# A mixer's products with ones and zeros, split into two float32r parts, and a looser order of weight splits

## The chip, the cores and the metric

The kernel runs on one core of a Trainium2 chip. The metric is the device time of one launch in microseconds; lower is better. TensorE multiplies, VectorE and ScalarE do elementwise work and read the products out of PSUM, SyncE issues nearly all loads from device memory.

## The reference

One transformer block on 256 tokens of width 2048, in float32, batch 1. A conditioning vector gives nine modulation vectors (`w_ada`). Three sublayers follow, each with a norm before and after and a residual: a gated feed-forward net (width 5632), a hybrid mixer, and a second feed-forward net. The mixer is

```python
p = h @ w_in
y_pool = multiscale_pool(p[..., :POOL_WIDTH], pool_w, pool_scale)
y_rwkv = rwkv7_time_mix(p[..., POOL_WIDTH:], mu_shift, w0, w2, a0, a2, g2, k_k, k_a, r_k, lnx_w, lnx_b)
return jnp.concatenate([y_pool, y_rwkv], axis=-1) @ w_out
```

`rwkv7_time_mix` has 24 heads of 64 channels. Sums over the 64 channels of a head occur three times: in the norm of `kk`, in the bonus (the sum of `r * k * r_k`, times `v`), and in the mean and variance of each head's output. Between them a recurrence runs over the tokens, with a state of 64x64 per head.

## The kernel before, in words

Tokens lie along the free dimension, channels on the 128 partitions; one 128-row tile holds two heads. Large products are made with weights in two float32r parts: `split` (L181) lets ScalarE copy a raw weight tile to `hi` (L187) and VectorE compute `lo = raw - hi` (L188); three matmuls, `hi` by the activation's high part, `hi` by its low part and `lo` by its high part, stand for one product (`mm3` L207, `rows_mm`). There are four `hi` and `lo` buffers in the mixer and four raw ones; a raw buffer is free for its next load when `lo` is made.

Other products of the mixer are plain float32. Four of them for each group multiply data of 128x512 by a constant of ones and zeros, so as to sum over the channels of a head (`blocks`) or over blocks of 8 (`same`): the norm (`ns`, from `sq`), the bonus (from `rk`), the diagonal of small triangular blocks (`same`, from `dg`), and the variance (in `rwkv_b`, from another `sq`). In the trace the first two write the bank `ga` from tiles named `y` and `t`, the third writes `sa` from `pm`, the fourth `sb` from `t`; all four read `consts`.

The recurrence is done in chunks of 64 tokens, for six groups of four heads. `rwkv_a` (L1117) prepares a group, `rwkv_b` (L1260) solves it; both are generators that yield at fixed places. `stage` (L931) runs 12 slots for each group: in each slot first two pieces of weight work (`pieces`: the projection of the next group, a piece being one split and its matmuls), then the end of the group before last (`b_old`), then a segment of `rwkv_b` for the previous group, a segment of `rwkv_a` for this group (slots 0, 2, 4, 5, 6, 7, 9), other tasks, and a part of the conditioning sums (`ada`). In `rwkv_a`, `sq` and `rk` are made in slot 0, the norm's product stands in slot 2, the bonus in slot 4, `dg` is made in slot 7 and multiplied in slot 9. TensorE's instructions are bound to exactly this order (`ordered`, `pe` L197); those of the other engines are ordered by a scheduler by priority and its own estimates, then each engine runs its list in order. `mark` names an operation that later `ada` sums have to follow.

After group 5 a last stage runs with `rwkv_b` alone, at 1.5 pieces a slot; these are pieces of `w_out` (six matmuls of 512 columns each). Only there `act_linked` is set: several copies of `rwkv_b` out of PSUM go through `link` (L385), and every later weight split's cast must follow the last of them:

```python
def link(self, op):
    if self.act_linked:
        self.act_link = op
    return op
...
    if self.act_link is not None:            # in split
        self.after(a, self.act_link, "order")
```

The linked copies are `Z0` (twice), `pm`, `X`, `Q` and the square before the variance, in slots 1, 3, 4, 5, 6 and 10. The bonus's result is read by `bv` (L1192), which frees bank `ga` for the matmuls `ga<-ar,bk` of the next slot; these need `ar` (L1181 and L1182).

Of the kernel before, what the change touches and what calls it, by code (L numbers as in the profile page):

```python
# [11 lines left out]
F32 = mybir.dt.float32  # L12
F32R = mybir.dt.float32r
AF = mybir.ActivationFunctionType
ALU = mybir.AluOpType
PSUM = bass.MemoryType.PSUM

P = 128
T = 256
# [23 lines left out]
C = 64  # L43
H = C // 2
NC = T // C
U = 2 * NC
B = 8
LOG_DECAY = -float(np.exp(-0.5))

CONST_LAYOUT = (("ident", P), ("quads", 32), ("blocks", P), ("center", C), ("tri", P), ("gmask", P),  # L50
                ("lmask", 2 * H), ("hmask", 2), ("eye", C), ("recip", 4 * 16),
                ("same", P), ("bmask", C // B), ("b32mask", H // B), ("imask", B))


def constant_pack():
    p, f = np.arange(P)[:, None], np.arange(P)[None, :]
    q, j = p % C, np.arange(C)[None, :]
    same = (p // C == f // C).astype(np.float32)
    levels = []
    o, i = p % H, np.arange(H)[None, :]  # L60
    for s in (8, 16):
        levels.append((o == i) | ((o // (2 * s) == i // (2 * s)) & (o % (2 * s) >= s) & (i % (2 * s) < s)))
    recip = np.concatenate([1.0 / np.minimum(np.arange(1, 17), w) for w in POOL_WINDOWS])
    parts = {
        "ident": p == f,
        "quads": p % 32 == np.arange(32)[None, :],
        "blocks": same,
        "center": (q == j) - 1.0 / C,
        "tri": same * (p <= f) * LOG_DECAY,
        "gmask": np.concatenate([q < j, q <= j], 1),  # L70
        "lmask": np.concatenate(levels, 1),
        "hmask": q // H == np.arange(2)[None, :],
        "eye": q == j,
        "recip": np.broadcast_to(recip, (P, 64)),
        "same": p // B == f // B,
        "bmask": q // B == np.arange(C // B)[None, :],
        "b32mask": p % H // B == np.arange(H // B)[None, :],
        "imask": q % B == np.arange(B)[None, :],
    }
    return np.ascontiguousarray(np.concatenate([parts[k].astype(np.float32) for k, _ in CONST_LAYOUT], 1))  # L80


class Block:
    def __init__(self, ctx, tc, I, out):
        self.ctx, self.tc, self.nc, self.I, self.out = ctx, tc, tc.nc, I, out
        pool = lambda name, bufs, **kw: ctx.enter_context(tc.tile_pool(name=name, bufs=bufs, **kw))
        self.const = pool("const", 1)
        self.big = pool("big", 1)
        self.accs = pool("accs", 1)
        self.small = pool("small", 2)  # L90
        self.dram = pool("dram", 2, space=bass.MemoryType.DRAM)
        self.sxx, self.rpre, self.rpost, self.xbias, self.ybias, self.xz, self.rzz, self.up = ({} for _ in range(8))
        self.uid = 0
        self.urgent = None
        self.gates = []
        self.act_link, self.act_linked = None, False
        self.ordered, self.pe_last = False, None

    def name(self, s):
# [96 lines left out]
    def pe(self, op):  # L196
# [4 lines left out]
            self.pe_last = op  # L201
        return op

    def mul(self, ps, a, b, start=True, stop=True):
        return self.pe(self.nc.tensor.matmul(ps, a, b, start=start, stop=stop))  # L205

# [12 lines left out]
    def warm(self, psum, n):  # L219

        ps = self.tile(psum, [P, 512], tag="mm")
        for _ in range(n):
            self.nc.tensor.matmul(ps, self.blocks, self.consts[:, :512], start=True, stop=True)

    def ada_begin(self, order):

# [158 lines left out]
    def link(self, op):  # L385

        if self.act_linked:
            self.act_link = op
        return op

    def in_order(self, ops):
# [466 lines left out]
    def mixer(self, ctx):  # L858
        nc, tc, I = self.nc, self.tc, self.I
# [19 lines left out]
        xa = self.tile(self.w1, [P, T], tag="xa")  # L879
        xg = self.tile(self.w1, [P, 2, T], tag="xg")  # L880
        nc.vector.memset(xw[C:C + 1, :], 1.0)
        last = []

        def lora(i, ps):
# [120 lines left out]
        n = NP // 2  # L1005
# [33 lines left out]
        bufs = {"t2": 3, "X": 1, "rhs": 1, "lg2": 1, "pm": 2}  # L1039
# [5 lines left out]
            pass  # L1045
        late(14, 15)
        self.ordered, self.pe_last = False, None
        self.act_link, self.act_linked = None, False
        for _ in pieces:
            pass  # L1050
        for q in range(3):
# [65 lines left out]
    def rwkv_a(self, st, g, r, k, v):  # L1117
# [4 lines left out]
        nc, mul = self.nc, self.mul  # L1122
# [6 lines left out]
        Wi, kk, sq, nrm = self.late  # L1129
# [3 lines left out]
        ps, pa = self.bank("sa"), self.bank("ga")  # L1133
# [11 lines left out]
            self.ln_exp(x, x, AF.Exp, scale=-1.0)  # L1145
        for i in range(2):
            nc.scalar.activation(half(sq, i), half(k, i), AF.Square, scale=self.column("k_k", js[i]))
        for i in range(2):
            nc.scalar.activation(half(kp, i), half(a, i), AF.Identity, bias=self.column("1-k_a", js[i]),
                                 scale=self.column("k_a", js[i]))  # L1150
        nc.vector.tensor_tensor(kp, kp, k, ALU.mult)
        rk = t1()
# [5 lines left out]
        L, ns = self.bank("sa"), self.bank("ga")  # L1158
        for i in range(2):
            for tt in range(2):  # L1160
                mul(L[:, i * T + tt * P:i * T + (tt + 1) * P], sg[:, (2 * tt + i) * P:(2 * tt + i + 1) * P], self.tri)
        mul(ns, self.blocks, sq)

        n2 = e[:, 4 * T:]
        nc.vector.tensor_scalar(n2, ns, 1e-24, None, ALU.max)
# [14 lines left out]
        nc.vector.tensor_tensor(bk[:, :, 1, :], ch(kk), ch(aw), ALU.mult)  # L1180
        nc.vector.tensor_tensor(ar[:, :, 0, :], ch(kk), W[:, :, :C], ALU.mult)  # L1181
        self.mark(nc.vector.tensor_tensor(ar[:, :, 1, :], ch(r), W[:, :, 1:], ALU.mult))  # L1182
        pairs = [[bk[hs[h], u, h:h + 2, :].rearrange("p a t -> p (a t)") for u in range(U)] for h in range(2)]
        wc = self.tile(self.w2p, [P, U, 1], tag="wc")
        nc.vector.tensor_copy(wc, W[:, :, C:])
# [1 line left out]


        ps = self.bank("ga")
        mul(ps, self.blocks, rk)  # L1190
        bv = self.tile(self.w2p, [P, 2 * T], tag="bv")
        nc.vector.tensor_tensor(bv, ps, v, ALU.mult)  # L1192

# [24 lines left out]
        for h in (1, 0):  # L1218
# [7 lines left out]
        comp = self.tile(self.w1, [P, U, B], tag="comp")  # L1226
        nc.vector.tensor_reduce(comp, ex.rearrange("p u b t -> p u t b"), mybir.AxisListType.X, ALU.add)
        dg = self.tile(self.w2p, [P, U, B, B], tag="pm")
        self.mark(nc.vector.tensor_tensor(dg, comp.unsqueeze(2).broadcast_to([P, U, B, B]),
                                          self.imask.unsqueeze(1).unsqueeze(3).broadcast_to([P, U, B, B]), ALU.mult))  # L1230

        bt = self.tile(self.w2p, [P, U, P], tag="bt")
        for h, tag in enumerate(("sa", "ga")):
# [4 lines left out]
        yield  # L1238

        ps = self.bank("sa")  # L1240
        mul(ps, self.same, dg.rearrange("p u s t -> p (u s t)"))
        ps = ps.rearrange("p (u s t) -> p u s t", u=U, s=B)
        x = self.tile(self.w1, [P, U, B], tag="x")
        nc.vector.tensor_copy(x, self.imask.unsqueeze(1).broadcast_to([P, U, B]))
        for s_ in range(B - 1):
            n = B - 1 - s_
# [13 lines left out]
    def rwkv_b(self, g, st):  # L1260
# [60 lines left out]
            mul(ps[dn[h], u], T1[up[h], u, H:], Z0[up[h], u])  # L1321
        pm = z("pm")
        for h in range(2):
            self.link(nc.scalar.copy(pm[dn[h]], ps[dn[h]]))
        X = self.tile(self.w2p, [P, U, C], tag="X", bufs=1)
        nc.vector.tensor_tensor(X.rearrange("p u (a t) -> p u a t", a=2), Z1.unsqueeze(2).broadcast_to([P, U, 2, H]),
                                self.hmask.unsqueeze(1).unsqueeze(3).broadcast_to([P, U, 2, H]), ALU.mult)
# [2 lines left out]
        for u, h in [(u, 1 - h) for u, h in units]:  # L1330
            mul(ps[up[h], u], pm[dn[h], u], Z1[dn[h], u])
        for h in range(2):
            self.link(nc.scalar.copy(X[up[h], :, H:], ps[up[h]]))
        yield


# [49 lines left out]
        self.link(nc.scalar.activation(sq, yp, AF.Square))  # L1386
        yield
        ps = self.bank("sb")
        mul(ps, self.blocks, sq)
        var, inv = t2(), t2()  # L1390
        self.rsqrt(inv, ps, var, sq, 1.0 / C, LN_EPS)
        for i in range(2):
# [40 lines left out]
    def begin_rest(self, mm):  # L1433

        nc, I = self.nc, self.I
        nc.sync.dma_start(self.consts[:, P + 32:], I["consts"][:, P + 32:])
        self.load_columns([("b_ada_tail", I["b_ada"][P * P:])] + [(n, I[n]) for n in ("a0", "k_a", "r_k", "lnx_w", "lnx_b")]
                          + [("mu_shift", I["mu_shift"][:38 * P]), ("mu_tail", I["mu_shift"][RWKV_IN - P:])], mm)
        self.col["b_ada"] += [(P + off, take, ct, at) for off, take, ct, at in self.col["b_ada_tail"]]
# [102 lines left out]
```

## Time and profile before

| | us |
|---|---|
| median of 3 runs (lowest, highest) | 2101.57 (2100.3, 2104.24) |
| the profiled execution | 2103.58 |
| its span | 2101.8 |
| busy in the span: TensorE, VectorE, ScalarE | 2057.7, 1600.0, 1009.0 |

The profile is one execution. A matmul's record lasts longer than the time to the next one, since matmuls overlap; how long one holds the engine is read from start to start. In brackets behind a row stands the idle time before it and what ended it. `PE` is TensorE, `PEld` its weight load, `DVE` VectorE, `ACT` ScalarE; `L205` is a line of the kernel, and as all ordered matmuls share that line, they are told apart by their tiles.

### The profile page before, as it was taken

How to read it: one execution, taken by the hardware profiler on the slowest of the kernel's cores; microseconds unless marked ns; L12 is line 12 of the kernel's file. 1: busy time of each engine (PE TensorE's matmuls, PEld its weight loads, DVE VectorE, ACT ScalarE, POOL GpSimd, SP SyncE). 2: the span in 40 equal slices, each digit the busy share in tenths (PEclk: the TensorE clock that was granted, in tenths of full speed). 3: DMA queues.
4: the chain of work that ended last, by engine and by line, in shares of the span. 5: the costliest groups of instructions: out<-in, count | busy, mean ns of one | idle time of the engine just before them, and what ended most of it. 6: DMA issues, size and time to landing. Idle time of an engine off the chain costs nothing. (4 is left out here: it accounts for less than half of the span.)

```text
span 2101.8 us, 39682 instructions
## 1 busy us (share of the span) xinstructions
PE 2057.7 (98%) x16395; PEld 1833.5 (87%) x16395; DVE 1600.0 (76%) x2210; ACT 1009.0 (48%) x1472; POOL 0.2 (0%) x4
## 2 busy tenths in 40 slices
PE   8999999999999999999999989999999999999998
PEld 5899999888888888998989867899998888888887
DVE  4898899878889977688888946876899655555556
ACT  4443345433444545765555634554354344443453
POOL 0000000000000000000000000000000000000000
PEclk9999999999999999999999999999999999999999
DMA  9999887799989956665555435686978755555553
GB/s 336 311 339 340 308 305 274 284 328 327 318 310 334 359 185 189 184 194 156 152 161 159 132 125 164 228 313 216 332 281 301 252 188 189 192 181 200 189 192 120
DMA packets 310691, 506.94 MB, mean 241 GB/s; under 512 B 14085, under 2 KB 160622, under 8 KB 309998
## 3 DMA queue, kind: packets, MB, share of 16 engines
q1 hardware_dynamic: 309020, 501.05, 69.8%
q10 hardware_dynamic: 1490, 3.36, 0.5%
q8 instruction: 128, 2.10, 0.4%
q14 instruction: 53, 0.43, 0.1%
HBM read 500.13 MB, written 4.22 MB: 240 GB/s over the span
## 5 line engine op out<-in xcount | busy, mean ns | idle before, releaser
L187 ACT CAST hi<-raw 128x1024 fp32r<-128x1024 f32 (+1 forms) x759 | 692.7, 917 | 837.5 <-PE mm L205 568.4
L188 DVE TENSOR_TENSOR lo<-raw,hi 128x1024 fp32r<-128x1024 f32 (+1 forms) x759 | 798.8, 1058 | 357.2 <-ACT hi L187 353.6
L205 PE MATMUL mm<-hT,hi 128*128 128x256 f32 x4160 | 756.5, 284 | 7.1 <-DVE hT L472 3.6
L205 PEld LDWEIGHTS mm<-hT,hi 128*128 128x128 f32 x4160 | 637.6, 188 | 23.6 <-issue 7.2
L205 PE MATMUL mm<-hT,lo 128*128 128x256 f32 x2080 | 579.0, 280 | 6.0 <-DVE lo L188 6.0
L216 PE MATMUL mm<-hT,hi 128*128 128x512 f32 x1280 | 448.5, 394 | 0.0
L205 PE MATMUL mm<-hi,act 128*128 128x512 f32 (+1 forms) x1328 | 399.6, 382 | 0.0
L205 PEld LDWEIGHTS mm<-hT,lo 128*128 128x128 f32 x2080 | 390.3, 188 | 7.1 <-DVE lo L188 7.0
L217 PE MATMUL mm<-hT,lo 128*128 128x256 f32 x1280 | 359.1, 281 | 0.0
L282 DVE SCALAR_TENSOR_TENSOR acc<-ada,csilu,acc 128x1024 f32<-128x1024 f32 (+1 forms) x240 | 299.5, 1248 | 38.3 <-DMA ada<-in_w_ada_dram 36.9
L216 PEld LDWEIGHTS mm<-hT,hi 128*128 128x128 f32 x1280 | 240.8, 188 | 56.0
L205 PEld LDWEIGHTS mm<-hi,act 128*128 128x128 f32 x1328 | 246.4, 188 | 48.1
L205 PE MATMUL mm<-lo,act 128*128 128x512 f32 (+1 forms) x664 | 253.3, 381 | 0.0
L217 PEld LDWEIGHTS mm<-hT,lo 128*128 128x128 f32 x1280 | 239.8, 187 | 0.1
L205 PEld LDWEIGHTS mm<-lo,act 128*128 128x128 f32 x664 | 124.8, 188 | 24.1
L715 DVE TENSOR_TENSOR act<-act,mm 128x512 f32<-128x512 f32 x144 | 97.3, 684 | 2.1 <-PE mm L205 1.2
L282 DVE SCALAR_TENSOR_TENSOR ada<-x,csilu,ada 128x512 f32<-128x512 f32 (+1 forms) x45 | 41.3, 917 | 0.1
L205 PE MATMUL mm<-hi,work 128*128 128x512 f32 x128 | 41.0, 391 | 0.0
L467 ACT ACTIVATE hT<-mm,mod,gs 128x256 fp32r<-128x256 f32 x48 | 27.1, 570 | 15.4 <-PE mm L205 15.3
L713 ACT COPY act<-mm 128x512 f32<-128x512 f32 x40 | 23.4, 586 | 19.2 <-PE mm L205 18.7
L750 ACT ACTIVATE silu<-silu 128x512 f32<-128x512 f32 x20 | 12.7, 633 | 37.1 <-DVE silu L749 37.1
L205 PE MATMUL mm<-hi,hT 128*128 128x512 f32 (+1 forms) x80 | 26.7, 388 | 3.8 <-ACT hi L187 3.8
(413 smaller groups left out, 1662.8 us busy)
## 6 DMA issues: line engine op xcount, KB each, us to landing
raw<-in_ffn_w_down_dram SPq DMA_DIRECT2D x88, 1024.0 KB, 5.1
raw<-in_ffn_w_gate_dram SPq DMA_DIRECT2D x80, 1024.0 KB, 7.8
raw<-in_ffn_w_up_dram SPq DMA_DIRECT2D x80, 1024.0 KB, 5.2
ada<-in_w_ada_dram SPq DMA_DIRECT2D x160, 512.0 KB, 6.9
ada<-in_w_ada_dram SPq DMA_DIRECT2D x192, 256.0 KB, 5.3
raw<-in_w_in_dram SPq DMA_DIRECT2D x80, 512.0 KB, 4.6
x<-in_w_ada_dram SPq DMA_DIRECT2D x64, 256.0 KB, 5.1
raw<-in_w_out_dram SPq DMA_DIRECT2D x32, 512.0 KB, 3.6
```

The costliest lines, as they stand in the source:

```text
L187: a = nc.scalar.copy(hi, raw)
L188: d = nc.vector.tensor_tensor(lo, raw, hi.bitcast(F32), ALU.subtract)
L205: return self.pe(self.nc.tensor.matmul(ps, a, b, start=start, stop=stop))
L216: nc.tensor.matmul(ps.rearrange("p a t -> p (a t)"), hi, x.rearrange("p a t -> p (a t)"), start=start, stop=False)
L217: nc.tensor.matmul(ps[:, 0, :], lo, x[:, 0, :], start=False, stop=stop)
L282: self.later(nc.vector.scalar_tensor_tensor(acc, raw[:, i], ck, acc, ALU.mult, ALU.add))
L467: a = nc.scalar.activation(self.hT[:, k, 0, :], ps[:, j, :], AF.Identity, scale=g, bias=sh)
L713: nc.scalar.copy(part, bank)
L715: nc.vector.tensor_tensor(part, part, bank, ALU.add)
L750: last = nc.scalar.activation(s, s, AF.Silu)
```

## The change

Three of the four products (`ns`, the bonus, `same`) get their data in two float32r parts, made by `two_parts`, and are done as two float32r matmuls by `mul2`. `blocks` and `same` move from the constants to a tile of their own, which is loaded at the start of the mixer and rounded to float32r by a copy. The variance keeps the float32 product. The parts take the buffers `t2` of `rwkv_b`. `warm` uses another constant. In the last stage a split's cast follows the linked copy before the last one; where two half copies were linked, one link remains.

```diff
+EXACT_LAYOUT = (("blocks", P), ("same", P))
...
+    def two_parts(self, x, high, low):
+        self.nc.scalar.copy(high, x)
+        op = self.nc.vector.tensor_tensor(low, x, high.bitcast(F32), ALU.subtract)
+        return high, low, op
+    def mul2(self, ps, const, high, low):
+        self.mul(ps, const, high, True, False)
+        self.mul(ps, const, low, False, True)
...
-            self.nc.tensor.matmul(ps, self.blocks, self.consts[:, :512], start=True, stop=True)
+            self.nc.tensor.matmul(ps, self.ident, self.consts[:, :512], start=True, stop=True)
...
         if self.act_linked:
-            self.act_link = op
+            self.act_link, self.act_next = self.act_next, op
...
+        exact, raw = self.tile(self.w1, [P, n], F32R, tag="exact"), self.tile(self.w2p, [P, n], tag="W", bufs=1)
+        nc.sync.dma_start(raw, I["consts"][:, width:width + n])
+        nc.vector.tensor_copy(exact, raw)
...
+        spare = lambda: self.tile(self.w2p, [P, 2 * T], F32R, tag="t2", bufs=3)
+        sq_parts = self.two_parts(sq, spare(), spare())[:2]
...
-        mul(ns, self.blocks, sq)
+        self.mul2(ns, self.blocks, *sq_parts)
...
         self.mark(nc.vector.tensor_tensor(ar[:, :, 1, :], ch(r), W[:, :, 1:], ALU.mult))
+        rk_parts = self.two_parts(rk, spare(), spare())[:2]
...
-        mul(ps, self.blocks, rk)
+        self.mul2(ps, self.blocks, *rk_parts)
...
-        self.mark(nc.vector.tensor_tensor(dg, comp.unsqueeze(2).broadcast_to([P, U, B, B]),
-                                          self.imask.unsqueeze(1).unsqueeze(3).broadcast_to([P, U, B, B]), ALU.mult))
+        nc.vector.tensor_tensor(dg, comp.unsqueeze(2).broadcast_to([P, U, B, B]),
+                                self.imask.unsqueeze(1).unsqueeze(3).broadcast_to([P, U, B, B]), ALU.mult)
+        *dg_parts, op = self.two_parts(dg.rearrange("p u s t -> p (u s t)"), spare(), spare())
+        self.mark(op)
...
-        mul(ps, self.same, dg.rearrange("p u s t -> p (u s t)"))
+        self.mul2(ps, self.same, *dg_parts)
...
         for h in range(2):
-            self.link(nc.scalar.copy(pm[dn[h]], ps[dn[h]]))
+            op = nc.scalar.copy(pm[dn[h]], ps[dn[h]])
+        self.link(op)
...
-        mul(ps, self.blocks, sq)
+        mul(ps, self.blocks.bitcast(F32), sq)
```

The copies of `X` are linked like those of `pm`.

## Rows read from the trace of the kernel before

**Rows 1.** The page's busy time: us, share of the span, instructions, by engine.
```profile
PE 2057.7 (98%) x16395; PEld 1833.5 (87%) x16395; DVE 1600.0 (76%) x2210; ACT 1009.0 (48%) x1472; POOL 0.2 (0%) x4
```

**Rows 2.** Busy time by stretches of the mixer.
```profile
core 0: us, PE busy (x) PEld busy (x) DVE busy (x) ACT busy (x) POOL busy (x), PEclk, DMA share, GB/s
926.56:989.06 62.50, 62.50 (x978) 56.35 (x977) 50.74 (x107) 34.45 (x65) 0.00 (x0) 1.00 0.50 152
1222.00:1283.00 61.00, 52.05 (x706) 38.47 (x704) 26.65 (x49) 22.59 (x45) 0.00 (x0) 0.94 0.37 121
990.10:1002.90 12.80, 12.80 (x234) 11.50 (x233) 12.55 (x23) 9.08 (x18) 0.00 (x0) 1.00 0.67 199
...
1240.00:1250.00 10.00, 6.74 (x53) 4.56 (x51) 3.31 (x6) 2.75 (x6) 0.00 (x0) 0.89 0.18 64
1250.00:1260.00 10.00, 7.19 (x97) 5.08 (x95) 1.89 (x3) 3.45 (x8) 0.00 (x0) 0.77 0.41 149
```

**Rows 3.** TensorE's timeline at group 2's products: start, length, line, tiles, count.
```profile
989.07 1.02 PE L205 MATMUL ga<-y,consts 128*128 128x512 f32 x2
...
990.17 0.28 PE L205 MATMUL mm<-hT,lo 128*128 128x256 f32 x1
...
990.52 0.28 PE L205 MATMUL mm<-hT,lo 128*128 128x256 f32 x1
...
997.21 1.12 PE L205 MATMUL ga<-t,consts 128*128 128x512 f32 x2
998.26 0.62 PE L205 MATMUL sa<-consts,v 64*64 64x64 f32 x14
...
1023.26 1.13 PE L205 MATMUL sa<-pm,consts 128*128 128x512 f32 x2
...
1024.46 0.28 PE L205 MATMUL mm<-hT,lo 128*128 128x256 f32 x1
```

**Rows 4.** TensorE's timeline in two slots of the last stage.
```profile
1227.94 0.50 PE L205 MATMUL sa<-hi,hT 128*128 128x512 f32 x1
1228.28 0.39 PE L205 MATMUL sa<-lo,hT 128*128 128x512 f32 x1
1228.51 0.40 PE L205 MATMUL sa<-hi,hT 128*128 128x512 f32 x1
...
1230.94 0.75 PE L205 MATMUL zb<-pm,Z 32*32 32x32 f32 x64
1232.68 0.49 PE L205 MATMUL sa<-hi,hT 128*128 128x512 f32 x1 [0.99 <-ACT hi L187]
1233.41 0.50 PE L205 MATMUL sa<-lo,hT 128*128 128x512 f32 x1 [0.23 <-DVE lo L188]
```

**Rows 5.** TensorE's waits, 1205 to 1300: total, times, longest.
```profile
PE mm L205 <- ACT hi L187: 3.8, 3, 1.5
PE sa L205 <- ACT hi L187: 3.2, 3, 1.3
```

**Rows 6.** ScalarE's timeline behind `zb<-pm,Z`.
```profile
1231.74 0.37 ACT L1313 COPY Z<-zb 128x256 f32<-128x256 f32 x1 [1.19 <-PE zb L205]
1232.01 1.66 ACT L187 CAST hi<-raw 128x512 fp32r<-128x512 f32 x3
```

**Rows 7.** Splits of 128x512 in the mixer: busy and mean; idle before, releasers.
```profile
L188 DVE TENSOR_TENSOR lo<-raw,hi 128x512 fp32r<-128x512 f32 x216 | 147.2, 688 | 69.6 <-ACT hi L187 68.7 <-PE zb L205 0.3
L187 ACT CAST hi<-raw 128x512 fp32r<-128x512 f32 x215 | 131.7, 618 | 124.3 <-PE mm L205 87.1 <-PE zb L205 11.6 <-issue 7.7
```

**Rows 8.** VectorE's and TensorE's timelines at the bonus's bank, group 2.
```profile
1002.21 0.69 DVE L1192 TENSOR_TENSOR bv<-ga,v 128x512 f32<-128x512 f32 x1
...
1002.99 0.37 PE L205 MATMUL ga<-ar,bk 64*128 64x128 f32 x1
```

**Rows 9.** TensorE's only wait between 860 and 1210.
```profile
PE ga L205 <- DVE ar L1181: 0.9, 1, 0.9
```

**Rows 10.** Loads of `w_out`: size, median us to landing; a wait for one.
```profile
raw<-in_w_out_dram SPq DMA_DIRECT2D x32, 512.0 KB, 3.6
...
ACT r L187 <- DMA raw<-in_w_out_dram: 3.3, 1, 3.3
```

More of the change, by code (lines that the diff above doesn't have):

```diff
@@ L48 @@
 LOG_DECAY = -float(np.exp(-0.5))
-CONST_LAYOUT = (("ident", P), ("quads", 32), ("blocks", P), ("center", C), ("tri", P), ("gmask", P),
+CONST_LAYOUT = (("ident", P), ("quads", 32), ("center", C), ("tri", P), ("gmask", P),
                 ("lmask", 2 * H), ("hmask", 2), ("eye", C), ("recip", 4 * 16),
-                ("same", P), ("bmask", C // B), ("b32mask", H // B), ("imask", B))
+                ("bmask", C // B), ("b32mask", H // B), ("imask", B))
+EXACT_LAYOUT = (("blocks", P), ("same", P))
 def constant_pack():
@@ L79, in constant_pack @@
     }
-    return np.ascontiguousarray(np.concatenate([parts[k].astype(np.float32) for k, _ in CONST_LAYOUT], 1))
+    return np.ascontiguousarray(np.concatenate([parts[k].astype(np.float32) for k, _ in CONST_LAYOUT + EXACT_LAYOUT], 1))
 class Block:
@@ L95, in __init__ @@
         self.gates = []
-        self.act_link, self.act_linked = None, False
+        self.act_link, self.act_next, self.act_linked = None, None, False
         self.ordered, self.pe_last = False, None
@@ L881, in mixer @@
         nc.vector.memset(xw[C:C + 1, :], 1.0)
+        width, n = (sum(w for _, w in layout) for layout in (CONST_LAYOUT, EXACT_LAYOUT))
+        exact, raw = self.tile(self.w1, [P, n], F32R, tag="exact"), self.tile(self.w2p, [P, n], tag="W", bufs=1)
+        nc.sync.dma_start(raw, I["consts"][:, width:width + n])
+        nc.vector.tensor_copy(exact, raw)
+        for i, (key, w) in enumerate(EXACT_LAYOUT):
+            setattr(self, key, exact[:, i * P:(i + 1) * P])
         last = []
@@ L1047, in mixer @@
         self.ordered, self.pe_last = False, None
-        self.act_link, self.act_linked = None, False
+        self.act_link, self.act_next, self.act_linked = None, None, False
         for _ in pieces:
@@ L1332, in rwkv_b @@
         for h in range(2):
-            self.link(nc.scalar.copy(X[up[h], :, H:], ps[up[h]]))
+            op = nc.scalar.copy(X[up[h], :, H:], ps[up[h]])
+        self.link(op)
         yield
@@ L1435, in begin_rest @@
         nc, I = self.nc, self.I
-        nc.sync.dma_start(self.consts[:, P + 32:], I["consts"][:, P + 32:])
+        width = sum(w for _, w in CONST_LAYOUT)
+        nc.sync.dma_start(self.consts[:, P + 32:], I["consts"][:, P + 32:width])
         self.load_columns([("b_ada_tail", I["b_ada"][P * P:])] + [(n, I[n]) for n in ("a0", "k_a", "r_k", "lnx_w", "lnx_b")]
```

## The prediction

> **What bounds the kernel now.** I read the page's table of engines first: TensorE is busy 98% of the span, VectorE 76%, ScalarE 48% [rows 1]. So time comes off where TensorE's instructions get shorter or where it stands idle; a shorter instruction elsewhere gives nothing. The change lies in the mixer, so I went on to busy time by stretches [rows 2]. In one whole period of a middle group (926.56 to 989.06, 62.5 us) TensorE shows no idle time and VectorE is busy 50.74 us, 81%. In the last stage (1222 to 1283) TensorE is busy only 52.05 of 61 us, and the granted clock averages 0.94. Those are two different problems, and the diff has a part for each.
>
> Then the matmul timeline at the three products [rows 3]. A product with ones and zeros is plain float32 and leaves two records. In group 2 the first starts at 989.07. The weight matmuls behind it go by threes, each `lo` 0.35 us after the one before (990.17, 990.52), so the first three would have started at 990.17 - 0.24 = 989.93: the product holds the engine 0.86 us. The second goes from 997.21 to 998.26, 1.05 us. The third, by the same reckoning, goes from 1023.26 to 1024.46 - 0.24 = 1024.22, 0.96 us. A float32r matmul of the same width takes 0.23 from start to start (1228.28 to 1228.51) [rows 4].
>
> Last, who waits in the last stage. The 61 - 52.05 = 8.95 us of idle time lie at six places, each a wait for `hi` of a weight split, 3.8 + 3.2 us in all [rows 5], followed by a shorter one for its `lo`. One place in full [rows 4, 6]: `zb<-pm,Z` starts at 1230.94; ScalarE copies its result at 1231.74, and only then come three casts in a row at 1232.01. The weight matmul behind `zb` on TensorE starts at 1232.68, after 0.99 us idle, and its `lo` matmul after another 0.23. It does not need the copy; the casts' data had been loaded, or three could not follow at once. The order put on ScalarE through `link` holds them back.
>
> **The change, part by part.**
>
> *Shorter products.* Each becomes two float32r matmuls. First: 0.86 becomes 2 x 0.23 = 0.47 (unrounded), 0.39 less. Second: 1.05 becomes 0.47 and some handover to the float32 blocks behind it, for which I leave 0.08: 0.50 less. Third: 0.96 becomes 0.47, but its first record is long because it follows smaller blocks, and that may stay: 0.39 to 0.49, I take 0.44. That is 1.33 us a group, 8.0 us for six groups. The fourth product (`sb<-t`) stays float32.
>
> *The parts.* Each product adds a ScalarE copy and a VectorE subtraction of 128x512. Splits of that shape cost 0.62 and 0.69 us [rows 7]. Per group that is 1.9 us on ScalarE and 2.1 on VectorE, which goes from 81% to about (50.74 + 2.07) / 61.2 = 86%. Averaged, that hides; locally each product needs a look. First: `sq` depends only on `k` and is made long before. Third: a whole slot of other work lies between `dg` and its product, against 0.62 + 0.69 us and two handovers. If this cover were gone, each would cost TensorE up to 1.3 us. Second is the tight one. VectorE is busy 12.55 of the 12.80 us from 990.10 to 1002.90 [rows 2], and the last thing there is `bv`, which frees the bank that `ga<-ar,bk` writes next: `bv` ends at 1002.90, the matmul starts at 1002.99 [rows 8]. VectorE has 0.25 us of slack. TensorE arrives 0.89 us earlier, VectorE's chain only 0.39 (it hangs on the first product), so 0.50 is missing, and the subtraction takes up to 0.69 more. The loss is 0.50 + 0.69 - 0.25 = 0.94 us at most, and 0.25 if the subtraction goes where an `ada` sum stood, which nobody awaits. I take 0.5 for five groups, 2.5 us, as the subtraction comes before `ada` in program order. In group 0 TensorE already idles 0.9 us for `ar` [rows 9]: of the 0.89 saved ahead of it only the 0.39 may pass on, and up to 0.69 is added. I take 1.2 lost (bounds 0.5 and 1.2).
>
> *Buffers.* The parts use the three `t2` buffers of `rwkv_b`, nine uses per stage. In order of use, each falls on a buffer whose last reader is a past product or the previous group's normalization. I cost it at nothing; the cover is the slot or more between them, and if it is missing, a part comes late as above.
>
> *The constants.* 128 KB are loaded in the mixer's opening and rounded by one VectorE copy. SyncE issues one DMA more, ahead of the first weights; the copy is short, but in VectorE's queue the chain of rows stands behind it which TensorE awaits there. If it stands in the queue before its data, it costs up to a load's landing, 3.6 us [rows 10]; if not, nothing. I take 0.3, nearer to hidden. `warm` only changes its stationary operand: nothing.
>
> *Splits follow the last but one copy.* Only the last stage has links. A cast then may go a whole slot earlier; there are four `hi` buffers for at most two pieces per slot. What goes is the 8.95 us of idle time. The records hide a bit more: from `hi` to its `lo` it is 0.73 us in the stalled place against 0.34 in a free one [rows 4], 0.39 lost where 0.23 shows, so 6 x 0.16 = 1.0. And after three such waits the granted clock falls, from 1.00 to 0.89 in 1240 to 1250 and 0.77 in 1250 to 1260 [rows 2]. That is (0.11 + 0.23) x 10 = 3.4 us of full clock, partly in idle time; I count 3.0, as without the waits nothing is left that precedes the fall from 2.4 to 1.2 GHz. Together 12.95.
>
> What is late next: the copies. `Z` takes 0.37 and starts at once when `zb` ends [rows 6]; the matmul that needs it stands behind one piece of 6 x 0.23 = 1.4 us, so it is ready. The two copies of `X` (2 x 0.37) with a cast just begun in front (0.62) take 1.4 too: no room. I leave one of six waits in place with its clock, about 2 us, and take 11 (bounds 0, if the new order frees nothing, and 13).
>
> *Sum.* 8.0 - 2.5 - 1.2 - 0.3 = 4.0, and 11: 15.0 us. The profiled execution took 2103.58 us (span 2101.8), so 2088.6; the median before, 2101.57, is 2.0 lower, so 2086.6.
>
> **Rivals.**
> VectorE takes over the middle groups. For: 98% busy in the tight window [rows 2]. Against: 19% idle over a period. If every subtraction lengthens its group, 6 x 2.07 = 12.4 us are added, the products' cut is not seen, and the last stage's 12.95 stays: 2101.6 - 0.5 = 2101.1. The Trainium skill's page "Perfetto Trace Analysis" (Identifying the Most-Contended Engine) says that occupancy is a fair measure of VectorE, while matmul busy time is not one of TensorE. By that rule the tight window is VectorE's; this trace agrees there (98%), not over the period (81%).
>
> The new order frees nothing: the casts would wait for something else, such as a `hi` buffer or a load. Then only 4.0 us come: 2097.6. Against: the casts at 1232.01 follow each other without a wait, so buffers and data were there.
>
> Slower: casts that now stand ahead of a copy wait for their load, and the copy waits behind them in ScalarE's queue. For: one cast waits 3.3 us for `w_out` [rows 10]. At each of six copies one landing of 3.6 us less the 1.4 that a piece covers is 2.2, 13.2 in all, beside the 8.95 that stay; with the clock loss doubled (3.0) it is +16.2 - 4.0 = +12.2: 2113.8. It decides from (4.2 + 4.0) / 6 + 1.4 = 2.8 us per copy. Against: a load waits for its buffer, which a held cast keeps; earlier casts bring earlier loads. The Trainium skill's page "TensorE: Matmul & The Clock Gate" (Architectural detail) calls ScalarE's queue strictly first in, first out; no run here shows yet whether a copy is caught behind a cast.
>
> **How the numbers follow.** Forecast 0.74, its own range 2079 to 2093: all good is 12.95 + 8.0 - 1.25 - 0.5 = 19.2, 2082.4, and 3 for what I don't see; all bad is 11 + 8.0 - 4.7 - 1.2 - 3.6 = 9.5, 2092.1, and a little of a second wait. Nothing freed 0.12, at 2097.6. VectorE 0.09, at 2101.1. Slower 0.05. A measurement of this kernel tells 0.2%, 4.2 us, from no change. 2097.6 lies near that edge, so I split that case: faster 0.74 + 0.08 + 0.02 (a mild VectorE case) = 0.84, same 0.11, slower 0.05. The range 2079 to 2098 leaves out VectorE's case, the slower one and a little below.
>
> **What would show it.** TensorE's idle time in the last stage falls from 8.95 to under 3 us, and the clock stays at 1.00. The products appear as two records some 0.23 apart. The group period falls from 62.5 to between 61.2 and 61.9; if it does not, VectorE took it, and `ga<-ar,bk` waits for `bv`. A copy of `Z`, `pm` or `X` that starts over 1.4 us after its bank is ready would show the slower case. A mixer that ends no earlier, or new TensorE waits of over 5 us between 860 and 1210, makes the prediction wrong.

## The result: 0.3% slower, and the profile after

The changed kernel takes 2109.57 us (median of 22 runs, 2099.26 to 2116.01), the kernel before 2102.53 beside it (22 runs): ratio 1.0029, 95% interval 1.0017 to 1.0042. The forecast was 2086.6, with 2098.0 as its upper end. The profiled execution took 2109.59 us, span 2107.8.

The engines' totals tell nothing: TensorE is as busy as before [rows 1], with each product shorter.

```profile
PE 2057.6 (98%) x16395; PEld 1841.6 (87%) x16395; DVE 1606.8 (76%) x2229; ACT 1017.7 (48%) x1490; POOL 0.2 (0%) x4
```

So I cut both traces at the same instructions on TensorE: the norm products at the start of a feed-forward net (`mm<-scale,x`), the first `sa<-consts,bk` of each group's slot 2, the first `y<-G,SV` of group 5 (in the last stage).

| stretch, us | before | after | difference |
|---|---|---|---|
| opening of the first net | 290.8 | 289.3 | -1.5 |
| rest of the first net | 509.5 | 515.6 | +6.1 |
| mixer up to group 0's slot 2 | 75.2 | 73.6 | -1.6 |
| group 0's slot 2 to group 1's | 50.1 | 60.4 | +10.3 |
| groups 1, 2, 3, 4 | 62.5, 62.5, 61.6, 61.6 | 63.0, 64.3, 61.0, 61.9 | +1.9 |
| group 5 and last stage up to `y<-G,SV` | 98.5 | 90.9 | -7.7 |
| rest of the mixer | 67.0 | 65.2 | -1.7 |
| second net | 762.4 | 762.6 | +0.2 |

Each column is one profile, and the stretches before the mixer vary by themselves: over the kernels below that leave the opening alone it takes 288.1 to 296.3 us, and the rest of the first net took 506.6 us in one that leaves it as it was. The last stage and what follows it won 9.4 us, and everything else lost more. TensorE's timeline shows the split products, in group 2 as in [rows 3] (bonus, then diagonal):

```profile
1010.55 0.74 PE L218 MATMUL ga<-t,exact 128*128 128x512 f32 x2
1011.22 1.15 PE L218 MATMUL sa<-consts,v 64*64 64x64 f32 x32
...
1039.18 0.73 PE L218 MATMUL sa<-t,exact 128*128 128x512 f32 x2
1039.75 0.40 PE L218 MATMUL mm<-hT,hi 128*128 128x256 f32 x2
```

The bonus holds TensorE for 1011.22 - 1010.55 = 0.67 us in place of 1.05, the diagonal for 0.57 in place of 0.96, and from the matmul before the norm's product to the one behind it 0.39 us are gone too: 1.16 us a group. The shorter products are real. What they ran into are TensorE's waits from 860 to 1210 (total, times, longest), where there had been one of 0.9 us [rows 9]. `W` L1191 is a 0.07 us memset that updates the same semaphore as `bv` just ahead of it; what the matmul needs is `bv`:

```profile
PE ga L218 <- DVE W L1191: 6.5, 4, 2.5
PE pb L218 <- DVE Z L1283: 2.4, 1, 2.4
PE ga L218 <- DVE bv L1216: 0.5, 1, 0.5
```

First place, group 0, bank `ga`: VectorE's timeline before and, below it, after, and the matmul that waited.

```profile
885.37 0.69 DVE L1174 TENSOR_TENSOR bk<-t,y 128x512 f32<-128x512 f32 x1
885.97 0.48 DVE L1177 SCALAR_TENSOR_TENSOR y<-k,cols,y 128x256 f32<-128x256 f32 x1
886.36 0.69 DVE L1192 TENSOR_TENSOR bv<-ga,v 128x512 f32<-128x512 f32 x1
886.96 0.69 DVE L1180 TENSOR_TENSOR bk<-y 128x512 f32<-128x512 f32 x1
887.56 0.69 DVE L188 TENSOR_TENSOR lo<-raw,hi 128x512 fp32r<-128x512 f32 x1
888.17 0.69 DVE L1181 TENSOR_TENSOR ar<-y,W 128x512 f32<-128x512 f32 x1
```

```profile
888.54 0.69 DVE L1197 TENSOR_TENSOR bk<-t,y 128x512 f32<-128x512 f32 x1
889.15 0.48 DVE L1200 SCALAR_TENSOR_TENSOR y<-k,cols,y 128x256 f32<-128x256 f32 x1
889.54 0.68 DVE L190 TENSOR_TENSOR lo<-raw,hi 128x512 fp32r<-128x512 f32 x1
890.15 0.68 DVE L1203 TENSOR_TENSOR bk<-y 128x512 f32<-128x512 f32 x1
890.75 0.68 DVE L1204 TENSOR_TENSOR ar<-y,W 128x512 f32<-128x512 f32 x1
891.35 0.68 DVE L190 TENSOR_TENSOR lo<-raw,hi 128x512 fp32r<-128x512 f32 x1
891.95 0.68 DVE L1216 TENSOR_TENSOR bv<-ga,v 128x512 f32<-128x512 f32 x1
...
892.69 0.58 PE L218 MATMUL ga<-ar,bk 64*128 64x128 f32 x1 [2.46 <-DVE W L1191]
```

In group 0 the scheduler's list itself changed: `bv` stood ahead of `ar` and now stands last, behind `ar` and another `lo`. Second place, in the second half of group 0: VectorE's loop over `x`, whose end `Z` TensorE awaits; before and, below it, after.

```profile
906.23 0.21 DVE L1248 TENSOR_TENSOR xt<-sa,x 128x56 f32<-128x56 f32 x1
...
911.31 0.44 DVE L1257 STREAM_TRANSPOSE Z<-Z 128x256 f32<-128x256 f32 x1
```

```profile
913.63 0.21 DVE L1274 TENSOR_TENSOR xt<-sa,x 128x56 f32<-128x56 f32 x1
913.76 0.68 DVE L209 TENSOR_TENSOR t<-y,t 128x512 fp32r<-128x512 f32 x1
914.36 0.68 DVE L190 TENSOR_TENSOR lo<-raw,hi 128x512 fp32r<-128x512 f32 x1
914.96 0.21 DVE L1276 TENSOR_TENSOR x<-x,xt 128x56 f32<-128x56 f32 x1
...
921.54 0.44 DVE L1283 STREAM_TRANSPOSE Z<-Z 128x256 f32<-128x256 f32 x1
...
922.04 0.75 PE L218 MATMUL pb<-Z,T 32*32 32x32 f32 x64 [2.36 <-DVE Z L1283]
```

L209 is the subtraction of group 1's norm: its `sq` is made in group 0's late slots. From the first `xt` to the end of `Z` the loop takes 8.35 us in place of 5.52. Only L209 (0.68) is new in it; the scheduler's list also puts three more `lo` and two operations on the next group's `v` between its steps, work that stood elsewhere before. Behind both waits TensorE's granted clock falls between its two levels, 2.4 and 1.2 GHz (windows as in [rows 2]; before, it was 1.00 throughout group 0, and in the changed kernel it is back at 1.00 from 900 to 910):

```profile
890.00:900.00 10.00, 7.54 (x46) 6.98 (x47) 4.64 (x9) 1.50 (x3) 0.00 (x0) 0.66 0.25 78
...
920.00:930.00 10.00, 7.96 (x111) 6.14 (x112) 6.67 (x15) 3.44 (x7) 0.00 (x0) 0.65 0.77 223
930.00:940.00 10.00, 10.00 (x204) 9.59 (x204) 6.06 (x11) 5.89 (x11) 0.00 (x0) 0.84 0.41 120
```

Third place, outside the mixer: the first net, near 300 us. ScalarE's timeline and TensorE's wait (`work` tiles are the columns that `load_columns` loads and TensorE transposes):

```profile
294.42 0.30 ACTq L145 DMA_DIRECT2D work<-in_lnx_b_dram  x1
300.21 0.58 ACTq L145 DMA_DIRECT2D work<-in_mu_shift_dram  x2
300.89 1.99 ACT L189 CAST hi<-raw 128x1024 fp32r<-128x1024 f32 x2 [6.79 <-DMA work<-in_mu_shift_dram]
...
303.97 0.29 PE L148 MATMUL mm<-consts,work 115*128 115x115 f32 x1 [4.01 <-DMA ada<-in_w_ada_dram]
```

Before, the two `mu_shift` loads were issued at 295.40 and the next cast began at 297.25. The constants' load of `begin_rest`, at 252 us, is now 534 columns wide in place of 790, and behind it (first at 281.56) the scheduler put SyncE's loads in another order. Loads share eight semaphores in rotation, and by the numbers in the records the `mu_shift` load now takes the one of the 1 MB load of `w_up` issued at 292.27, so ScalarE waits for that to land. The Trainium skill's page "TensorE: Matmul & The Clock Gate" (Architectural detail) calls ScalarE's queue strictly first in, first out; this trace agrees: 6.79 us without a cast.

### The profile page after: what moved, and what is told of

Its sections match the earlier page's. It is cut to its first block, busy times and chain, and to the rows that moved or that the text cites. A ratio compares the mean times of both kernels' runs of the same rounds, so it can differ in the third digit from the quotient of the medians.

```text
span 2107.8 us, 39736 instructions
## 1 busy us (share of the span) xinstructions
PE 2057.6 (98%) x16395; PEld 1841.6 (87%) x16395; DVE 1606.8 (76%) x2229; ACT 1017.7 (48%) x1490; POOL 0.2 (0%) x4
## 5 line engine op out<-in xcount | busy, mean ns | idle before, releaser
L218 PEld LDWEIGHTS mm<-hi,work 128*128 128x128 f32 x128 | 24.0, 188 | 5.0
```

## The experiments

Theory: (1) the order of splits works; (2) the shorter constants' load costs the first net some 6 us through ScalarE's queue; (3) single subtractions and the place of `bv` in VectorE's list make TensorE wait, and the clock makes group 0 dear. Rivals: the first net is chance; VectorE's load as a whole is what costs. Line numbers shift by a few between kernels.

**The order of splits alone** (the kernel before, with `act_link, act_next = act_next, op` and one link for two half copies).

> The kernel before with the looser order of the last stage's splits and nothing else. Theory: the order of splits does what it was meant to do, and the loss lies in the other parts. In the changed kernel the stretch from group 5's gates to the last stage's end shrank by 7.7 us and the stretch behind it by 1.7; with this part alone the time falls by 8 to 9.5 us (ratio 0.9955 to 0.9965), no TensorE wait of over 0.5 us for hi or lo is left in the last stage, and the mixer's groups 0 to 4 take what they took before. Rival: the shorter stretch came from the split products and not from the order; then the time changes by less than 3 us (ratio over 0.9985).

2095.14 against 2102.72 us, ratio 0.9962 (0.9949 to 0.9976). TensorE's waits from 1205 to 1300, and then one window between the same two instructions (the first `y<-G,SV` of group 4 and of group 5), in the kernel before and in this one:

```profile
PE pb L205 <- ACT X L1334: 2.3, 1, 2.3
PE ga L205 <- ACT y L1091: 0.6, 1, 0.6
```

```profile
1213.68:1272.41 58.73, 50.65 (x708) 37.82 (x707) 25.60 (x57) 19.62 (x39) 0.00 (x0) 0.94 0.34 115
```

```profile
1211.83:1265.27 53.44, 50.53 (x709) 39.05 (x708) 27.11 (x60) 21.52 (x42) 0.00 (x0) 0.90 0.39 126
```

All waits for `hi` are gone; one for the copies of `X` is left. Idle time in the window falls from 8.08 to 2.91 us, but the clock does not rise: it is 0.94 before and 0.90 here. The mixer falls from 539.1 to 531.4, and groups 0 to 4 are as before. Theory 1 holds. What holds the copies of `X` is no cast. ScalarE's queue stands on a load, `G<-g`, which reads back what `g<-grow` writes and waits for that to land:

```profile
1247.88 0.87 ACTq L509 DMA_DIRECT2D G<-g  x2
1248.79 0.74 ACT L1334 COPY X<-zb 32x256 f32<-32x256 f32 x2 [5.34 <-DMA g<-grow]
```

Before, the same load was issued at 1246.29 and the copies came at 1251.54 without a wait for it; in the changed kernel ScalarE idles 5.16 us for it ahead of them.

**The products without it.**

```diff
-            self.act_link, self.act_next = self.act_next, op
+            self.act_link = op
...
```

> The changed kernel with the old order of splits in the last stage (constants and split products stay). Theory: products and constants together lose what the order of splits wins back: +6.0 and +9.4 give +15 us on the time before (ratio 1.007); group 0 again takes some 60 us from its gates to those of group 1 (before 50.1). Rival (the order of splits gives nothing by itself): +6 us, ratio 1.003, as the changed kernel.

2121.71 us, ratio 1.0081 (1.0061 to 1.0101): +17 us by the ratio, 19 by the medians; group 0 takes 59.1. As the theory has it.

**The constants alone** (all four products plain, old links).

```diff
...
-        self.mul2(ns, self.blocks, *sq_parts)
+        mul(ns, self.blocks.bitcast(F32), sq)
...
```

> The changed kernel without the order of splits and with all three products in plain float32 as before; what is left is the move of blocks and same: a shorter load of constants in the first feed-forward net, a load and a rounding copy at the start of the mixer. Theory: the shorter load moves the order of the loads in the first net, ScalarE's queue stands on the last load of columns, TensorE idles 4 us there and runs at a lower clock after it; the mixer starts at about 804.8 as in the changed kernel (before 800.3), and the time is 4 to 5 us over that before (ratio 1.002). Rival: the late mixer start was chance in one profiled execution; then it starts at 800 to 801 and the time changes by under 1 us.

2110.83 us, ratio 1.0038 (1.0024 to 1.0053). In the profile the mixer starts at 806.9; groups 0 to 4 take 50.1, 62.5, 62.5, 61.6, 61.6. Chance is out: the move of the constants costs 8 us by itself, more than expected. (That it is the shorter load in it that moves SyncE's order is argued, not shown: no run changes that load alone.) The profiled run, 4 us under the median of its kernel, shows 5.6 us of it behind the opening of the first net (515.1 for 509.5) and a mixer that is 1.6 us shorter (537.5).

**The bonus, the norm, the diagonal plain in turn** (the rest as changed; the bonus's `rk_parts` dropped and `mul(ps, self.blocks.bitcast(F32), rk)` in place of `mul2`, the others alike; norm and diagonal have one run each).

> The changed kernel with the bonus's product in plain float32 again (norm and diagonal stay split). Theory: the bonus's subtraction, put ahead of bv in VectorE's full queue, makes TensorE wait 2.5 us for bank ga in group 0 and the clock falls behind it; without it that wait is at most 1 us, group 0 falls from 60.4 to 50 to 52 us, the cut of six bonus products (at most 0.5 us each) is given up, and the time is 6 to 9 us under that of the changed kernel, level with the kernel before (ratio 0.999 to 1.001). Rival: VectorE as a whole is too full, whichever subtraction it is; then a third of the loss goes, 3 us, and group 0 still takes over 56 us.

> The changed kernel with the norm's product in plain float32 again (bonus and diagonal stay split). What is read is group 0 (before 21.7 + 28.4 us in its two halves; changed kernel 25.3 + 35.0; without the bonus's parts 22.5 + 35.0). Theory: in the second half, group 1's norm subtraction (0.68 us, from tile y) stands in the middle of VectorE's loop over x, for whose last result Z TensorE waits 2.4 us, and the clock falls behind that wait. Without it Z is ready about 0.7 us sooner, the wait is 1.0 to 1.8 us, and the second half takes 29 to 34 us, depending on whether the clock still falls; the first half stays at 25. Rival: VectorE's whole list got later and no single subtraction matters; then the second half stays at 35.

> The changed kernel with the diagonal's product in plain float32 again (norm and bonus stay split). Theory as for the norm: the diagonal's parts come between dg and the bank that the loop over x reads, one copy and one subtraction (1.3 us) sooner without them, but its product is 0.5 us longer: Z is ready 0.5 to 1 us sooner, the wait of 2.4 us shrinks to 1.4 to 1.9, the second half of group 0 takes 30 to 35 us, the first stays at 25. Rival (the whole list is late): 35.

| | halves of group 0 | groups 1 to 4 | us |
|---|---|---|---|
| before | 21.7, 28.4 | 62.5, 62.5, 61.6, 61.6 | 2102.5 |
| changed | 25.4, 35.0 | 63.0, 64.3, 61.0, 61.9 | 2109.6 |
| bonus plain | 22.4, 35.0 | 61.7, 61.7, 60.8, 60.8 | 2101.9, ratio 0.9995 (0.9983 to 1.0007) |
| norm plain | 22.5, 29.2 | 62.0, 62.0, 60.9, 60.9 | 2095.4 |
| diagonal plain | 24.0, 28.3 | 64.7, 63.2, 61.4, 62.3 | 2103.8 |

The total without the bonus came as expected, group 0 did not: it takes 57.4 us, over the 56 of the rival. I had put its whole loss down to the bonus, but its second half stayed at 35.0. That half is dear only while norm and diagonal are both split. With the norm plain the loop over `x` takes 7.25 us and TensorE waits 1.2 for `Z`; with the diagonal plain it takes 5.53, as before the change, and TensorE does not wait at all, more than I had thought. The rival (the whole list is late) is out for this half. The first half, too, fell with the norm plain, to 22.5 where I expected 25. With the diagonal plain TensorE waits the same 2.5 us there, and the 24.0 goes with a clock of 0.83 from 890 to 900 in place of 0.66. The clock: four fences with TensorE's waits in group 0 and the windows of its halves, first with the bonus plain, then with the norm plain:

```profile
PE pb L218 <- DVE Z L1282: 2.4, 1, 2.4
PE ga L218 <- DVE ar L1204: 2.0, 1, 2.0
```

```profile
882.20:904.70 22.50, 20.52 (x199) 18.91 (x197) 18.73 (x35) 11.30 (x22) 0.00 (x0) 1.00 0.48 135
904.70:939.60 34.90, 32.55 (x443) 29.98 (x442) 27.37 (x59) 19.34 (x36) 0.00 (x0) 0.85 0.64 190
```

```profile
PE ga L218 <- DVE ar L1203: 2.0, 1, 2.0
PE pb L218 <- DVE Z L1282: 1.2, 1, 1.2
```

```profile
877.85:900.31 22.46, 20.49 (x199) 18.86 (x197) 18.97 (x35) 11.85 (x22) 0.00 (x0) 1.00 0.47 133
900.31:929.55 29.24, 28.01 (x443) 26.36 (x442) 26.59 (x58) 19.36 (x36) 0.00 (x0) 1.00 0.76 228
```

Here waits of 1.2 and 2.0 us leave the clock at 1.00 and cost less than they last; a wait of 2.4 costs 6.6 us (35.0 - 28.4), 4.2 more than it lasts, with the clock at 0.85 over that half.

**Split products from group 1 on, the norm's from group 2 on.**

```diff
-        sq_parts = self.two_parts(sq, spare(), spare())[:2]
+        sq_parts = self.two_parts(sq, spare(), spare())[:2] if g > 1 else None
...
```

> The changed kernel with the split products only from group 1 on, the norm's (whose parts are made within the group before) from group 2 on; group 0 is then, in every engine's order, as before the change. Theory: group 0 goes back from 60.4 to 50.1 us, the other groups and the first net stay as in the changed kernel, some 0.4 us is lost at group 1's norm: 10 us less than the changed kernel, 2099 to 2101 (ratio 0.998 to 0.999). Rival: the place moves and the loss does not vanish; the first group with split products then takes over 66 us in place of 63, and the time stays over 2105.

2098.78 us, ratio 0.9984 (0.9969 to 0.9999). Group 0 takes 50.1, groups 1 to 4 62.0, 62.8, 61.0, 63.4: the loss does not move on to the next group. This run shows one thing more. In group 1 the bonus is split and the norm still plain, and TensorE waits 0.1 us for `ga`; in groups 2 and 4, with both split, it waits 1.35. The kernel with the norm plain has at most 0.1 in all of groups 1 to 4. So in these groups the bonus's subtraction by itself costs next to nothing. With the norm split as well, it has to wait on VectorE until TensorE has done the norm's product (VectorE idles 0.33 us for it in group 2 of the changed kernel). By the kernel, that product reads one of the three `t2` buffers that the parts share; no run gives them a fourth buffer, so this reason is not shown.

**The same, bonus plain, all columns loaded from SyncE's queue.**

```diff
-                nc.scalar.dma_start(st[at:at + take, :],
+                nc.sync.dma_start(st[at:at + take, :],
```

> As the last one, with the bonus in plain float32 in all groups, and the loads of columns in the first net issued on SyncE's queue in place of ScalarE's. Theory: without the bonus the groups 1 to 4 take 61.8, 61.8, 60.9, 60.9 (as measured without the bonus's parts, 7.3 us lost in group 0 alone), group 0 takes 50.1; ScalarE's queue no longer stands on a load's semaphore, so TensorE's wait of 3 to 5 us in the first net goes and the mixer starts within 2 us of 800: 2101.9 - 7.3 + 0.4 - 6 = 2089 (ratio 0.9935). Rival for the first net: the later loads, and not ScalarE's queue, make TensorE wait; then the mixer starts at 804 or later and the time is about 2095.

2092.32 us, ratio 0.9964 (0.9947 to 0.9982): 3 us short of the forecast. The mixer took 524.0 (539.1 before). Why the median is 3 us short stays open: the one profile is that of the slowest run (2103.86 us), where the mixer starts at 811.4 and not within 2 us of 800, as the opening and the first net's second half lost time. The stretch around 300 us no longer does: between the casts at 282 and 319 us it loses 0.3 us against the kernel before; the nine kernels with moved constants and ScalarE's columns lost 4.2 to 7.3.

**ScalarE's queue by itself**: the constants alone, and the kernel before, both with the first net's columns on SyncE (those of the opening stay on ScalarE).

> The kernel with the moved constants alone (8.1 us slower than before), with the loads of columns of the first feed-forward net issued on SyncE's queue in place of ScalarE's. Theory: those 8 us come from ScalarE's queue, which stands on the last load of columns and holds back the casts behind it; between the casts at 282 and 319 us seven kernels with the shorter constants lost 4.4 to 7.3 us, and one with its columns on SyncE 0.4. So here that stretch loses under 1 us and the time is 2103 to 2106, ratio 1.000 to 1.0015. Rival: the reordered loads behind it are what costs; then the time stays at 2109 to 2112 (ratio over 1.003).

> The kernel before with the same columns on SyncE's queue and nothing else: a control. Theory: its ScalarE queue never stood on such a load, so there is nothing to cure, ratio 0.9990 to 1.0010. Rival: SyncE's queue is hurt by the added loads (in one profile with them 4 to 5 us were lost between 550 and 600 us); then ratio 1.002 or more.

The first: 2106.03 us, ratio 1.0014 (1.0003 to 1.0024), 4.8 less than with ScalarE's columns, and the stretch at 300 us loses 0.3. In its profile ScalarE's next cast begins at 298.15, with no load in between; TensorE's wait of 2.8 us there is gone:

```profile
296.25 0.60 ACT L484 ACTIVATE work<-mm,mod,gs 128x256 f32<-128x256 f32 x1
298.15 1.05 ACT L189 CAST hi<-raw 128x1024 fp32r<-128x1024 f32 x1 [1.30 <-PE mm L218]
```

The control: 2104.52 us, ratio 1.0009 (0.9996 to 1.0022). Theory 2 holds for some 5 of the 8 us. The other 3 stay open: the control's interval (-0.8 to +4.6 us) allows that the loads on SyncE cost them.

**`bv` ahead in VectorE's list**, on the kernel with late splits (one run) and on the changed kernel.

```diff
-        nc.vector.tensor_tensor(bv, ps, v, ALU.mult)
+        with self.tc.high_priority(1000):
+            nc.vector.tensor_tensor(bv, ps, v, ALU.mult)
```

> As the kernel with split products from group 1 on (groups 1 to 4: 62.0, 62.8, 61.0, 63.4 us), with bv moved ahead in VectorE's order, five places before where it stood; nothing is left out. Theory: in the middle groups the bonus's subtraction makes bank ga late because bv stands last in a full stretch of VectorE; with bv first the waits for ga shrink from 2.7 us to under 1 and groups 1 to 4 take 61 to 61.8 us each, as without the bonus's parts or better. Rival: VectorE's whole load up to ar and bv counts, and ar is late in bv's place; then the groups stay at 62 to 63 us and TensorE waits for ar.

> The changed kernel, whole, with bv alone moved ahead in VectorE's order; nothing else. Theory: the loss in the first half of group 0 (25.4 us for 21.7) and the missing gain of groups 1 to 4 are the place of bv in VectorE's order and not its load: the first half of group 0 falls to 22 to 23.5 us, groups 1 to 4 take 61.7, 61.6, 60.7, 60.7; the second half of group 0 (35.0 us, the loop over x) and the first net stay as they are. That is 3 + 5.5 us off 2109.6: 2100 to 2103. Rival: in group 0 ar and bv wait for VectorE's load whatever their order; then the first half stays at 25 and the time at 2104 to 2106.

Groups 1 to 4 take 61.7, 61.6, 60.7, 60.7 in the one (2097.24 us, a single run) and 61.8, 61.6, 60.7, 60.7 in the other. On the changed kernel: 2103.59 us, ratio 1.0003 (0.9992 to 1.0014), a little over the 2103 of the theory, as group 0's first half only fell to 24.3. Its list of waits from 860 to 1210:

```profile
PE ga L218 <- DVE ar L1204: 2.7, 1, 2.7
PE pb L218 <- DVE Z L1284: 2.3, 1, 2.3
```

So in group 0 the rival is right: `ar` is late in `bv`'s place, as the load counts there. In the middle groups the place is enough: group 2's full window of [rows 2], placed alike behind its slot 2, in the changed kernel, with the matmul that follows and the 10 us behind the window, and in the last fence with `bv` ahead:

```profile
1003.85:1016.65 12.80, 12.17 (x231) 11.15 (x229) 12.60 (x25) 9.32 (x20) 0.00 (x0) 1.00 0.71 203
```

```profile
1017.38 0.37 PE L218 MATMUL ga<-ar,bk 64*128 64x128 f32 x1 [1.35 <-DVE W L1191]
```

```profile
1016.65:1026.65 10.00, 9.27 (x118) 8.83 (x119) 4.68 (x10) 2.54 (x5) 0.00 (x0) 0.83 0.30 70
```

```profile
1004.99:1017.79 12.80, 12.69 (x239) 11.66 (x239) 12.59 (x25) 8.84 (x18) 0.00 (x0) 1.00 0.67 201
```

VectorE is as full in both (12.60 and 12.59 us). TensorE waits 1.35 us in the one, of which 0.63 fall into the window, and the clock falls behind it; in the other it waits 0.11 us and the clock stays. The group takes 64.3 or 61.6. Groups 1 and 4 have the same wait of 1.35 without the fall, and take 63.0 and 61.9. The Trainium skill's page "Perfetto Trace Analysis" (Identifying the Most-Contended Engine) would name VectorE by its occupancy in both; here that measure can't tell them apart.

**What helped, together.**

> The looser order of splits; the norm's product split from group 2 on, the diagonal's from group 1 on, the bonus plain; moved constants; the columns of the first net on SyncE's queue, those of the opening on ScalarE's as before. Theory: mixer 524 us (before 539.1), first net as before within 3 us: 2087 to 2091 (ratio 0.9935 to 0.9955), under both kernels and under the order of splits alone (2095.1). Rival: columns on SyncE cost 4 us later in the first net as they did in one profile; then about 2093 to 2096.

> All that helped, together: the looser order of splits, the three split products (norm from group 2 on, the others from group 1 on), bv ahead in VectorE's order, the columns of the first net on SyncE's queue. Theory: mixer 524.5 us as in the run with ScalarE's columns, first net 4 us sooner than there: 2089 to 2093 (ratio 0.994 to 0.9955), level with the kernel that leaves the bonus plain. Rival: the bonus's split with bv ahead is worth more than its profile showed; then under 2088.

Without the bonus's parts 2092.77 us, ratio 0.9948 (0.9934 to 0.9962), 2 us over what I expected. With them and `bv` ahead 2091.85, ratio 0.9945 (0.9929 to 0.9961), as expected; the mixer takes 524.9, but the first net behind its opening (513.4) is 1 us shorter than with ScalarE's columns (514.5), not 4. Both beat the kernel before and the changed one; against the order of splits alone (0.9962) the intervals overlap, so what the split products add to it at best is not shown.

## Why the prediction was wrong

- **Shorter products, 8.0 us: right as a mechanism, mis-sized.** They save 1.16 us a group, 7.0 in all: the bonus 0.38 in place of 0.50, the others 0.39 each. Where little waits (`bv` ahead), groups 1 to 4 gain 0.7 to 1.0 us (62.5 to 61.8 and 61.6, 61.6 to 60.7), not 1.33; they lie where "between 61.2 and 61.9" would have them.
- **The subtraction in the bonus's slot, 2.5 us in five groups: mis-sized, 4.6 us of waits.** TensorE waits 1.35 us for `ga` in groups 1, 2 and 4, 0.5 in group 3 and 0.1 in group 5; my worst case was 0.94. `bv` stood last there before as well [rows 8]. The step that failed is the 0.39 us by which VectorE's chain was to start earlier: `bk<-ga` starts 2.10 us behind the group's first product in place of 2.05, as the bonus's subtraction stands ahead of it, and one more `lo` stands ahead of `bv`. So TensorE is ready 0.72 us earlier and starts 0.63 later. "Buffers: nothing" has its part in this, since that subtraction waits for the norm's product; how large a part is not shown. With `bv` ahead, groups 1 to 4 take 5.4 us less (63.0 + 64.3 + 61.0 + 61.9 less 61.8 + 61.6 + 60.7 + 60.7), 2.7 of them in group 2, where the clock had fallen.
- **Group 0, 1.2 us, "bounds 0.5 and 1.2": the step that failed most, 10.3 us.** I looked at the bonus's bank only and kept the order of VectorE's list. That order is the scheduler's: it put `bv` behind `ar` and more work into the loop over `x`. Norm ("made long before") and diagonal ("a whole slot lies between") were called covered, and together they delayed `Z`. And I priced waits by their length: the waits of group 0 grew by 3.9 us (2.46 + 2.36 less 0.88), and the rest of the 10.3 goes with the lower clock behind them. I had used the clock in the last stage's favour and not against the added waits.
- **Constants, 0.3 us, bound 3.6: failed, 8 us.** I priced the load that the mixer adds and not the first net, where the same edit shortens a load and the order of the later loads changed. Some 5 us of the 8 are ScalarE's queue standing on a load; the cause of the rest stays open.
- **Order of splits, 11 us: right, mis-sized.** Alone it gave 7.6 us. Idle time went as forecast but for one wait, 2.3 us, for the copies of `X`. That the forecast left about 2 us there was luck: I had put it down to a cast in front of the copies, and it is a load on ScalarE's queue. What failed is the 3.0 us of clock: between the same instructions it is 0.90 in place of 0.94, and I had taken the waits for `hi` as all that precedes its fall.
- **Rivals.** "The new order frees nothing" is out. "Casts wait ahead of copies" is out as told, though its sign came: the copies of `X` start 3.0 us after `zb`'s last matmul in the changed kernel (1260.49 to 1263.45), behind a load and not behind casts. "VectorE takes over the middle groups" was nearest, for another reason: the order of its list, not its 86%. No rival reached the first net.
- In sum 8.0 - 2.5 - 1.2 - 0.3 + 11 became, by the parts measured alone, about +4 (products in groups 1 to 5 with `bv` ahead) - 5 (`bv`) - 10 (group 0, its own products included) - 8 (constants) + 8 (order), some -11; measured -7.0. The intervals of the constants (5.0 to 11.1 us) and of the order (5.0 to 10.7) leave room for the difference.

## What to carry to other kernels

Where a scheduler lists the instructions, an edit changes the list as well as the load: price it by the place of the instruction that somebody waits for, and try a priority before giving up the edit. An edit of a load can reorder the loads behind it and cost more, elsewhere, than the edited place wins. A load issued on a compute engine's queue is an instruction in that engine's list: look at what stands behind it. Price a new wait on TensorE with the clock behind it.

## What the runs showed of the hardware

- In group 0, waits of 1.2 and 2.0 us left TensorE at 2.4 GHz; with waits of 2.4 and 2.5 us the clock fell to 1.2 GHz for a while (0.65 and 0.66 granted on average over the 10 us at them), and a wait of 2.4 cost 6.6 us in all. The length of a wait does not decide it alone: of the changed kernel's three waits of 1.35 us for `ga`, that of group 2 goes with a fall (0.83 over 10 us) and those of groups 1 and 4 do not (1.00). The one of 2.1 us for `X` in its last stage goes with 0.83.
- A load issued on ScalarE's queue held its casts for 6.79 us in the first net, though they had nothing to do with that load; another kept ScalarE idle for 5.16 us ahead of the copies of `X`.
- A 128x512 product by a constant holds TensorE in group 2 for 0.55 to 0.67 us as two float32r matmuls, against 0.86 to 1.05 as one in float32.
